# Instance normalization over long rows: 8 MB tiles in three buffers, loads and stores in one fixed order on one queue

## The chip, the cores and the metric

One core of one Trainium2 chip. Times are device microseconds (us) of one execution; a median is over the runs of one kernel. The work is the same in both kernels, so a lower time is better. I call "ring" the line of transfers that one issuing engine has handed to the core's 16 DMA engines; q1 in the profile is SyncE's, q10 ScalarE's. In profile lines DVE is VectorE, ACT ScalarE, POOL GpSimd and SPq the queue of SyncE.

## The reference

```python
# x: (256, 256, 4096) float32
mean = np.mean(x, axis=2, keepdims=True)
var = np.var(x, axis=2, keepdims=True)
return ((x - mean) / np.sqrt(var + eps)).astype(np.float32)
```

65,536 rows of 16 KB are read once and written once: 1073.7 MB each way.

## The kernel before

Each tile is 128 partitions x 2 rows (4 MB), in six buffers. SyncE issues the loads, ScalarE the stores.

```python
K = 2
BUFS = 6
x_t = x_flat.rearrange("(t p k) d -> t p k d", p=P, k=K)
# ... out_t likewise; pools io (BUFS), small (2 * BUFS), singles
for i in range(ntiles):
    x_tile = io.tile([P, K, d], mybir.dt.float32)
    nc.sync.dma_start(out=x_tile, in_=x_t[i])
    # ... stats, mv, rstd, nbias from the pool small
    for r in range(K):
        for j in range(nsub):                       # nsub = 8 pieces of 512
            nc.vector.bn_stats(out=stats[:, r, j, :], in_=xr[:, r, j, :])
        nc.vector.bn_aggr(out=mv[:, r, :], in_=stats[:, r])
    # ... one square root, reciprocal and bias product for both rows
    for r in range(K):
        nc.scalar.activation(out=x_tile[:, r, :], in_=x_tile[:, r, :], func=Identity,
                             bias=nbias[:, r : r + 1], scale=rstd[:, r : r + 1])
    nc.scalar.dma_start(out=out_t[i], in_=x_tile)
```

## Time and profile before

| | before |
|---|---|
| time, median of the first three runs | 5180.87 us (5179.3 to 5187.5) |
| VectorE, ScalarE busy | 51%, 38% |
| 16 DMA engines busy | 99.2% of the span |
| bytes moved over the span | 415 GB/s |

### The profile page before, as it was taken

What the parts mean: (1) busy time and instruction counts of PE and PEld (TensorE: products, weight loads), DVE (VectorE), ACT (ScalarE), POOL (GpSimd) and SP (SyncE); (2) the same over time, 40 slices, a digit from 0 to 9 for tenths busy, and PEclk for the clock granted to TensorE, in tenths of its full rate; (3) what the DMA queues carried; (4) which work ended last, traced back from release to release, by engine and by line L of the source; (5) the groups of instructions that cost most, each with busy time, mean ns of one, the idle gap of its engine ahead of it and who ended that gap; (6) DMA issues with size and microseconds to landing.
All of it is one profiled execution on the core that took longest, in us unless ns stands there. A gap on an engine that the chain in (4) does not pass through costs nothing.

```text
span 5180.7 us, 7450 instructions
## 1 busy us (share of the span) xinstructions
DVE 2654.0 (51%) x5121; ACT 1967.0 (38%) x769; POOL 0.2 (0%) x4
## 2 busy tenths in 40 slices
DVE  6544555554455555444555554455555445555543
ACT  3333333433333433433343433333343333334334
POOL 0000000000000000000000000000000000000000
DMA  9999999999999999999999999999999999999998
GB/s 425 412 410 413 420 417 422 417 414 416 410 416 413 417 418 414 413 412 417 417 416 418 413 414 418 410 417 420 417 415 417 417 413 417 417 419 415 415 416 367
DMA packets 73786, 2147.99 MB, mean 415 GB/s; under 512 B 8192, under 2 KB 8192, under 8 KB 8192
## 3 DMA queue, kind: packets, MB, share of 16 engines
q1 hardware_dynamic: 36864, 1073.76, 49.7%
q10 hardware_dynamic: 36864, 1073.76, 49.5%
q14 instruction: 58, 0.48, 0.0%
HBM read 1073.74 MB, written 1073.74 MB: 415 GB/s over the span
## 4 chain that ended last, share of the span: by engine, by line
DMA 69%; DVE 17%; ACT 7%; issue 6%; another core or an unknown queue 0%; SPq 0%
DMA x_tile<-in_x_dram 43%; DMA out_dram<-x_tile 26%; DVE stats L55 16%; ACT x_tile L77 7%; DVE mv L56 1%; DVE nbias L67 0%; SPq L46 0%; DVE rstd L65 0%; ACT rstd L58 0%
## 5 line engine op out<-in xcount | busy, mean ns | idle before, releaser
L55 DVE BATCH_NORM_STATS2 stats<-x_tile 128x6 f32<-128x512 f32 x4096 | 2464.1, 674 | 2460.3 <-DMA x_tile<-in_x_dram 2460.3
L77 ACT ACTIVATE x_tile<-x_tile,nbias,rstd 128x4096 f32<-128x4096 f32 x512 | 1917.8, 3793 | 3172.3 <-DVE nbias L67 3172.3
L56 DVE BATCH_NORM_AGGREGATE mv<-stats 128x2 f32<-128x48 f32 x512 | 185.7, 363 | 8.8
L58 ACT ACTIVATE rstd<-mv,eps_tile 128x2 f32<-128x2 f32 x256 | 71.7, 280 | 23.9 <-DVE mv L56 23.9
L67 DVE SCALAR_TENSOR_TENSOR nbias<-mv,rstd 128x2 f32<-128x2 f32 x256 | 41.0, 160 | 8.8
L65 DVE RECIPROCAL rstd<-rstd 128x2 f32<-128x2 f32 x256 | 27.7, 108 | 23.6 <-ACT rstd L58 23.6
L58 ACT ACT_TABLE_LOAD x1 | 1.3, 1283 | 0.7 <-PEq L101 0.7
L42 DVE MEMSET eps_tile<- 128x1 f32 x1 | 0.1, 59 | 0.8 <-PEq L101 0.8
L101 POOL MEMSET const-bfloat16-1.0<- 128x1 bf16 x1 | 0.1, 101 | 0.0
L101 POOL MEMSET const-uint8-127<- 128x1 uint8 x1 | 0.1, 101 | 0.0
L101 POOL MEMSET const-float32-0.0<- 128x1 f32 x1 | 0.1, 98 | 0.2 <-issue 0.2
L101 POOL MEMSET const-float32-1.0<- 128x1 f32 x1 | 0.1, 98 | 0.0
## 6 DMA issues: line engine op xcount, KB each, us to landing
x_tile<-in_x_dram SPq DMA_DIRECT2D x256, 4096.0 KB, 23.7
out_dram<-x_tile ACTq DMA_DIRECT2D x256, 4096.0 KB, 18.6
```

The lines of the kernel that those rows point to most:

```text
L42: nc.vector.memset(eps_tile, eps)
L55: nc.vector.bn_stats(out=stats[:, r, j, :], in_=xr[:, r, j, :])
L56: nc.vector.bn_aggr(out=mv[:, r, :], in_=stats[:, r])
L58: nc.scalar.activation(out=rstd, in_=mv[:, :, 1], func=mybir.ActivationFunctionType.Sqrt, bias=eps_tile, scale=1.0,)
L65: nc.vector.reciprocal(out=rstd, in_=rstd)
L67: nc.vector.scalar_tensor_tensor(out=nbias, in0=mv[:, :, 0], scalar=-1.0, in1=rstd, op0=mybir.AluOpType.mult, op1=mybir.AluOpType.mult,)
L77: nc.scalar.activation(out=x_tile[:, r, :], in_=x_tile[:, r, :], func=mybir.ActivationFunctionType.Identity, bias=nbias[:, r : r + 1], sca ...
L101: nc = _bacc.Bacc("TRN2", target_bir_lowering=False, num_devices=1)
```

## The change

Its intent: long runs in one direction, 64 KB contiguous per partition, and an order of transfers that doesn't depend on which of two rings happens to be served. Rows are finished one by one, and the store of a tile stands in SyncE's queue between two loads.

```diff
-    K = 2
-    BUFS = 6
+    K = 4
+    BUFS = 3
+    AHEAD = 2
...
+    def row(x_tile, r):      # statistics, rstd, nbias and normalization of one row
...
+    def finish(i):
+        x_tile = tiles.pop(i)
         for r in range(K):
-            nc.scalar.activation(... nbias[:, r : r + 1], scale=rstd[:, r : r + 1])
-        nc.scalar.dma_start(out=out_t[i], in_=x_tile)
+            row(x_tile, r)
+        nc.sync.dma_start(out=out_t[i], in_=x_tile)
+
+    for i in range(AHEAD):
+        load(i)
+    for i in range(ntiles):
+        finish(i)
+        if i + AHEAD < ntiles:
+            load(i + AHEAD)
```

More of the change, by code (lines that the diff above doesn't have):

```diff
@@ L25 @@
     n, d = x_flat.shape
-    rows_per_tile = P * K
-    assert n % rows_per_tile == 0
-    ntiles = n // rows_per_tile
+    ntiles = n // (P * K)
+    assert n == ntiles * P * K
     x_t = x_flat.rearrange("(t p k) d -> t p k d", p=P, k=K)
     out_t = out_flat.rearrange("(t p k) d -> t p k d", p=P, k=K)
-    BN_FMAX = nc.vector.BN_STATS_FMAX
-    nsub = (d + BN_FMAX - 1) // BN_FMAX
-    assert d % BN_FMAX == 0
+    FMAX = nc.vector.BN_STATS_FMAX
+    nsub = d // FMAX
+    assert d == nsub * FMAX
     io = ctx.enter_context(tc.tile_pool(name="io", bufs=BUFS))
-    small = ctx.enter_context(tc.tile_pool(name="small", bufs=2 * BUFS))
+    small = ctx.enter_context(tc.tile_pool(name="small", bufs=8))
     singles = ctx.enter_context(tc.tile_pool(name="singles", bufs=1))
@@ L42, with load @@
     nc.vector.memset(eps_tile, eps)
-    for i in range(ntiles):
+    tiles = {}
+    def load(i):
         x_tile = io.tile([P, K, d], mybir.dt.float32)
         nc.sync.dma_start(out=x_tile, in_=x_t[i])
-        stats = small.tile([P, K, nsub, 6], mybir.dt.float32)
-        mv = small.tile([P, K, 2], mybir.dt.float32)
-        rstd = small.tile([P, K], mybir.dt.float32)
-        nbias = small.tile([P, K], mybir.dt.float32)
+        tiles[i] = x_tile
+    def row(x_tile, r):
         xr = x_tile.rearrange("p k (s f) -> p k s f", s=nsub)
-        for r in range(K):
-            for j in range(nsub):
-                nc.vector.bn_stats(out=stats[:, r, j, :], in_=xr[:, r, j, :])
-            nc.vector.bn_aggr(out=mv[:, r, :], in_=stats[:, r])
+        stats = small.tile([P, nsub, 6], mybir.dt.float32)
+        mv = small.tile([P, 2], mybir.dt.float32)
+        rstd = small.tile([P, 1], mybir.dt.float32)
+        nbias = small.tile([P, 1], mybir.dt.float32)
+        for j in range(nsub):
+            nc.vector.bn_stats(out=stats[:, j, :], in_=xr[:, r, j, :])
+        nc.vector.bn_aggr(out=mv, in_=stats)
         nc.scalar.activation(
             out=rstd,
-            in_=mv[:, :, 1],
+            in_=mv[:, 1:2],
             func=mybir.ActivationFunctionType.Sqrt,
@@ L68 @@
             out=nbias,
-            in0=mv[:, :, 0],
+            in0=mv[:, 0:1],
             scalar=-1.0,
@@ L74 @@
         )
-        for r in range(K):
-            nc.scalar.activation(
-                out=x_tile[:, r, :],
-                in_=x_tile[:, r, :],
-                func=mybir.ActivationFunctionType.Identity,
-                bias=nbias[:, r : r + 1],
-                scale=rstd[:, r : r + 1],
-            )
-        nc.scalar.dma_start(out=out_t[i], in_=x_tile)
+        nc.scalar.activation(
+            out=x_tile[:, r, :],
+            in_=x_tile[:, r, :],
+            func=mybir.ActivationFunctionType.Identity,
+            bias=nbias,
+            scale=rstd,
+        )
+    def finish(i):
+        x_tile = tiles.pop(i)
+        for r in range(K):
+            row(x_tile, r)
[6 more added lines that the diff above has]
+            load(i + AHEAD)
 _INS = ['x', 'eps']
```

## The prediction

> **What bounds the kernel now.** I read the busy shares and the queue part of the page first, because they say which resource is full; then the waits, to see whether anything but that resource is waited for; then stretches of time, to see where the full resource is not at its best; last the packet records of the trace, one by one.
>
> ```profile
> DVE 2654.0 (51%) x5121; ACT 1967.0 (38%) x769; POOL 0.2 (0%) x4
> ...
> DMA  9999999999999999999999999999999999999998
> ...
> q1 hardware_dynamic: 36864, 1073.76, 49.7%
> q10 hardware_dynamic: 36864, 1073.76, 49.5%
> ...
> HBM read 1073.74 MB, written 1073.74 MB: 415 GB/s over the span
> ```
>
> VectorE and ScalarE are half idle. The 16 DMA engines are busy 49.7 + 49.5 = 99.2% of the span: q1 carries the loads (issued by SyncE), q10 the stores (issued by ScalarE). 2147.5 MB have to move and neither kernel can move less. So the time can fall only in two ways: the 0.8% in which engines are idle, or a shorter busy time per byte. A busy share of 99% doesn't say that the second is exhausted.
>
> ```profile
> ACT x_tile L77 <- DVE nbias L67: 3172.3, 256, 27.9
> DVE stats L55 <- DMA x_tile<-in_x_dram: 2460.3, 254, 23.9
> ...
> SPq L46 <- DMA out_dram<-x_tile: 4914.6, 248, 33.2
> ```
>
> VectorE waits for loads, and SyncE's queue (second view, the queue's own waits) waits 248 times for a store to land and free a buffer. Six buffers are always full: compute isn't the limit, and each load starts just when a store has ended. That last point matters below.
>
> ```profile
> 12.00:31.00 19.00, 17.55 (x33) 7.30 (x3) 0.00 (x0) 1.00 1.02 442
> ...
> 5126.00:5140.00 14.00, 6.15 (x15) 7.68 (x3) 0.00 (x0) 1.00 0.00 0
> 5141.00:5179.00 38.00, 0.65 (x4) 22.00 (x8) 0.00 (x0) 1.00 1.00 428
> 100.00:5100.00 5000.00, 2581.18 (x4979) 1896.61 (x742) 0.00 (x0) 1.00 0.99 416
> ```
>
> These are stretches of the trace; the last column is GB/s. The steady part runs at 416 GB/s, while the opening loads (no store about) and the closing stores (no load about) run faster. (442 is too high by the granularity of packets that straddle the window's ends.) Between 5126 and 5140 us nothing moves: the last loads' compute is waited for.
>
> **Packets.** The trace's DMA records list 65,536 data packets of 32 KB, each with a duration. The commonest by far is 1213 ns: 56,182 packets are within 3 ns of it, for loads, stores, and stretches where each engine alternates load, store, load. In the opening, where six loads stand in line on one ring, the completion write of one load follows that of the one before by 9.681 us on each engine: 8 packets, 433 GB/s over 16 engines, with no gap at the border of two DMAs. The floor of this program at that pace is 512 DMAs of 4 MB x 9.681 = **4957 us**. The difference to 5181 I account for so: the sum of all durations above 1213 ns, divided by 16, is 164 us (156 of it in 4,636 packets that took 1.75 us on average), and the time in which fewer than 16 packets are in flight is 61 us, of which 14.6 are the hole before 5141, some 3.5 the start and the end, and about 42 short gaps. 4957 + 164 + 61 = 5182.
>
> When do the long packets come? Lined up on the issues, nearly all lie 4 to 8 us after a load or a store was issued, as its first packets start. The first store of all is issued at 31.5 us; the loads of all 16 engines average 1803 ns at 34.0 us, the store packets begin at 35.3, and from then on load and store packets alternate at 1213. Around 2012 us a load joins a stretch with stores only, and the store packets then average 2057 ns. But a load issued at 2026.8, while the previous load was still on that ring, begins at 2034 with no long packet. So I read the cost as that of a ring that starts from empty beside a busy one, not as that of changing direction: around 2016 to 2023 nearly all 16 engines change direction together every packet and stay at 1213.
>
> **What the Trainium skill says.** (1) "DMA: Bandwidth & Descriptors", section "Measured", gives 425 GB/s for 16 MB transfers, and "Where 436 GB/s comes from" a ceiling of 435.2. The trace's 433 inside runs of loads agrees; 416 over the steady part is the gap that can be had, 4%. (2) The same page, "Queues, rings and completion order": every engine goes round-robin between the rings that have work, packet by packet. The trace agrees (alternation of q1 and q10). It names no cost for a ring that wakes up; the 164 us are this case's. (3) "Perfetto Trace Analysis", section "DMA Optimizations", advises loads on one issuing engine and stores on another, which the kernel does and the change undoes; nothing in this trace shows a gain from it while the buffers are all full.
>
> **The change, part by part.**
> *One ring.* All 256 issues of 8 MB go through SyncE. The built order is: three loads, two stores, then load, store, load, store. Store i waits for the compute of tile i; load i+2 stands behind it and waits for store i-1. Does the ring run empty? Let load i land at T. Store i-1 then runs T to T+19.4, load i+1 from there to T+38.7. Compute of tile i: a row takes 5.11 us of VectorE (16 statistics and 2 aggregates took 13.02 to 23.24 us, halved), plus its reciprocal and bias product, together about 5.4; four rows 21.6; then square root, reciprocal, product and the last 3.8 us activation, about 4.9. So store i is issued at T+26.5, 12 us before the ring would be empty, and load i+2 directly after, because store i-1 landed at T+19.4. A store's first packet needs some 4 us after issue (31.5 to 35.3). 12 covers it, so the ring never empties after the opening and each DMA starts behind a running one. By the reading above, that removes most of the 164 us and the 42 of short gaps.
> *Fewer, larger DMAs.* 256 rather than 512, and perhaps 64 KB packets. With 6 ns lost at a border this is worth next to nothing itself.
> *Compute.* ScalarE makes 512 square roots rather than 256 (256 x 0.28 = 72 us more), VectorE 512 more small operations of 0.11 to 0.16 us (about 70 us). Both lie beside the transfers: 21.5 us of VectorE per tile against 38.7 of DMA.
> *Ends.* Start 2.2 us as before. At the end the last load lands at T, store 126 ends at T+19.4, store 127 is issued at T+26.5 and moves about 1.5 us later: a hole of 8.6 us, then 19.4 and 1.3 to finish. Before, the hole was 14.6.
> *Sum.* Loads 256 x 9.681 = 2478; stores at the 9.725 us that the closing stores took, 2490; together 4968. Plus 2.2 + 8.6 + 1.3 = 4980. I add 8 us for remnants of long packets at 255 changes of direction (0.03 us each). **4988 us**, 3.7% less.
>
> **Rivals.** *A: the long packets belong to the change of direction after all.* Measured there: load joining stores about 1.1 us, store joining loads 0.6. With 128 of the first and 127 of the second, 217 us come back: 4980 + 217 = 5197, the same time. For it: every long stretch I looked at is also where the direction mix changes. Against: the free alternation and the free start at 2034. A half way (0.3 us per change) makes 5057. *B: the fixed order starves the ring.* SyncE issues in order, so a late store holds up a load that could go. If compute took 12 us more, each lost us would cost 128; VectorE's and ScalarE's durations vary by far less. At an overrun of 1 us: 5108. *C: 64 KB rows suit the memory worse, or lose to a coarser split.* Partition starts move from 32 to 64 KB apart; the profile before can't tell; 1% would be 50 us. *D: hidden anyway.* The engines are 99% busy, so no gain but the end's 6 us: 5175. This takes the busy share for efficiency, and the packets speak against it.
>
> **Range and chances.** The floor with its ends is 4957 + 12 = 4969, a little less if packets of 64 KB save something; I set the low end at 4962. The threshold of 2% is 5077. I give my reading, with up to 0.1 us per change, about 72%; a part of A (0.1 to 0.35 us) or C some 14%, still under 5077; A in full, B or D 13%; slower needs A and B together, 1%. So 0.86 / 0.13 / 0.01, range 4962 to 5075.
>
> **What would show it.** Right: GB/s of 428 to 433 in every slice between the ends, packets at twice 1213 ns (or still 1213) with hardly any long ones, all bytes on q1, SyncE's queue waiting mostly for ScalarE's last activation, idle time of VectorE about 18 us per tile, a hole of 8 to 9 us before the last store. Wrong: a dip or long packets at every change of direction (A), moments without any packet in each tile (B), all packets longer by a per cent (C). The prediction fails if the ring does empty, or if the first packet after a change of direction waits for the end of the one before.

## More of the kernel before

All runs told here were fast runs by the state recorded with them, and the granted clock was 1.000.

From the page of the kernel before: the data rate in 40 equal slices of the span, and the row of DMA queue 14 (packets, MB, share).

```profile
GB/s 425 412 410 413 420 417 422 417 414 416 410 416 413 417 418 414 413 412 417 417 416 418 413 414 418 410 417 420 417 415 417 417 413 417 417 419 415 415 416 367
...
q14 instruction: 58, 0.48, 0.0%
```

The first slice, which holds the only long stretch of loads without stores, is the fastest; those after it, but for the last, lie 2.5 to 5.3% below the 433 that the prediction works out for undisturbed packets.

## The result, and the profile after

| | before | after |
|---|---|---|
| median of 4 runs each | 5180.09 us | 5016.2 us (5007.2 to 5019.7) |
| ratio | | 0.966, 95% interval 0.962 to 0.970 |
| rate over the span | 415 GB/s | 428 GB/s |

Ratios here and below are the mean time of one kernel's fast runs over that of the other's in the same rounds, so not quite the ratio of the medians. The predicted time was 4988 us with a range of 4962 to 5075; the measured one is 28 us above the prediction.

The page of the changed kernel (the same parts as before):

```profile
span 5018.0 us, 7844 instructions
...
DVE 2667.3 (53%) x5633; ACT 2083.6 (42%) x1025; POOL 0.2 (0%) x4
...
GB/s 426 432 432 432 433 433 434 434 434 433 427 432 429 426 432 430 427 434 427 427 427 432 428 426 433 429 427 429 430 428 427 428 432 427 427 432 428 427 432 362
...
q1 hardware_dynamic: 36864, 2147.50, 99.7%
q14 instruction: 61, 0.50, 0.0%
HBM read 1073.74 MB, written 1073.74 MB: 428 GB/s over the span
```

All data is on q1. After the first slice and up to 1250 us (ten slices) the rate is 432 to 434 GB/s; the prediction had 428 to 433 for every slice between the ends. Then it varies from 426 to 434. The waits of the compute engines and of SyncE's queue (waiter, what it waited for, us in total, times, longest):

```profile
ACT rstd L60 <- DVE mv L59: 2483.6, 130, 36.6
DVE stats L58 <- DMA x_tile<-in_x_dram: 2228.2, 126, 34.6
```

```profile
SPq L88 <- ACT x_tile L76: 3233.2, 128, 26.6
SPq L88 <- DMA x_tile<-in_x_dram: 1631.0, 126, 20.5
SPq L48 <- DMA out_dram<-x_tile: 22.3, 2, 12.2
```

SyncE's queue no longer waits for stores to land (22 us against 4915 before). It waits for ScalarE to finish a tile, as predicted. One tile in the timeline of the changed kernel, start and duration of each:

```profile
2035.80 5.44 DVE L58 BATCH_NORM_STATS2 stats<-x_tile 128x6 f32<-128x512 f32 x9 [17.35 <-DMA x_tile<-in_x_dram]
...
2057.41 3.80 ACT L76 ACTIVATE x_tile<-x_tile,nbias,rstd 128x4096 f32<-128x4096 f32 x1 [0.42 <-DVE nbias L68]
2061.24 0.34 SPq L88 DMA_DIRECT2D out_dram<-x_tile  x1
2061.67 0.38 SPq L48 DMA_DIRECT2D x_tile<-in_x_dram  x1
```

From the load's landing to the store's issue: 2061.2 - 2035.8 = 25.4 us, where 26.5 was predicted. Stretches of time (busy times of the engines, granted clock, DMA share, GB/s):

```profile
100.00:1000.00 900.00, 477.28 (x1007) 367.99 (x182) 0.00 (x0) 1.00 1.00 433
1500.00:4900.00 3400.00, 1808.27 (x3820) 1411.63 (x695) 0.00 (x0) 1.00 1.00 429
4978.00:4997.00 19.00, 13.82 (x30) 15.96 (x7) 0.00 (x0) 1.00 0.11 48
4998.00:5016.00 18.00, 0.00 (x0) 0.00 (x0) 0.00 (x0) 1.00 0.94 408
```

The hole before the last store is 19 us long, more than twice what was predicted, and 0.11 of DMA share shows that a few engines still worked in it.

**Where the 28 us are.** Three quantities of the packet records account for a span: what the packets take undisturbed, what they take above that ("long packets", summed and divided by 16), and the time for which packets are missing ("gaps": 16 less the packets in flight, summed over time and divided by 16). The prediction calls its 61 us of this "the time in which fewer than 16 packets are in flight"; counted in that way it would be 155 us, but its sum is right with the 61. Packets are now 64 KB and take 2418 ns; one 8 MB DMA follows another by 19.32 us where nothing disturbs.

| term, us | predicted | measured |
|---|---|---|
| 256 DMAs, undisturbed | 4968 | 4946 |
| start and end | 3.5 | 3.1 |
| long packets | 8 | 50 |
| hole before the last store and other gaps | 8.6 | 20 |
| sum | 4988 | 5019 (span 5018.0) |

The profiled run took 5019.7 us, a little more than the median, so these terms differ by 31 us and not by 28.

**Engines drift apart.** The long packets lie almost all at the border of two DMAs (after 1250 us, 91% of their time is in the last packet of the earlier one), and only 6 of the 50 us come before 1250 us. I followed each DMA engine through the records (which don't name it) by joining the end of each packet to the start of the next. In the records each engine ends its part of a DMA with a packet of 4 bytes; I call it the completion write, and the distance from the first of the 16 to the last the lag. After the first load the lag is 0.5 us. After 300 us one engine is 5 us behind the first one, after 1250 us 11 to 12 us, and there it stays to the end; about nine engines remain within 0.5 us of each other. 12 us is just the slack of the fixed order. A load has landed only when the slowest engine has written its part (where VectorE waited for a load it started 0.3 to 0.5 us after the last completion write, and in the median 12.3 us after the first), so the store of that tile is issued late for the fast engines: from 1250 us on a store was issued in the median 1.2 us before the fastest engine ran out of work. Two questions follow, which the experiments take up: what drove the 164 us of long packets before, and what makes an engine lag.

### The profile page after: what moved, and what is told of

Read it like the earlier page. It is cut to its first block, busy times and chain, and to the rows that moved or that the text cites. A ratio compares the mean times of both kernels' runs of the same rounds, so it can differ in the third digit from the quotient of the medians.

```text
span 5018.0 us, 7844 instructions
## 1 busy us (share of the span) xinstructions
DVE 2667.3 (53%) x5633; ACT 2083.6 (42%) x1025; POOL 0.2 (0%) x4
## 3 DMA queue, kind: packets, MB, share of 16 engines
q1 hardware_dynamic: 36864, 2147.50, 99.7%
## 4 chain that ended last, share of the span: by engine, by line
DVE 45%; another core or an unknown queue 43%; ACT 9%; DMA 1%; issue 1%; ACTq 0%
DVE stats L58 41%; ACT x_tile L76 9%; DVE mv L59 2%; DMA x_tile<-in_x_dram 1%; DVE rstd L67 1%; DVE nbias L68 1%; ACT rstd L60 1%; ACTq L60 0%
## 5 line engine op out<-in xcount | busy, mean ns | idle before, releaser
L58 DVE BATCH_NORM_STATS2 stats<-x_tile 128x6 f32<-128x512 f32 x4096 | 2506.3, 674 | 2228.2 <-DMA x_tile<-in_x_dram 2228.2
L76 ACT ACTIVATE x_tile<-x_tile,nbias,rstd 128x4096 f32<-128x4096 f32 x512 | 1945.7, 3800 | 403.5 <-DVE nbias L68 403.5
L60 ACT ACTIVATE rstd<-mv,eps_tile 128x1 f32<-128x1 f32 x512 | 148.8, 291 | 2508.5 <-DVE mv L59 2483.6
L67 DVE RECIPROCAL rstd<-rstd 128x1 f32<-128x1 f32 x512 | 74.8, 146 | 87.5 <-ACT rstd L60 87.3
L68 DVE SCALAR_TENSOR_TENSOR nbias<-mv,rstd 128x1 f32<-128x1 f32 x512 | 75.2, 147 | 4.3
```

The lines of the kernel that those rows point to most:

```text
L58: nc.vector.bn_stats(out=stats[:, j, :], in_=xr[:, r, j, :])
L60: nc.scalar.activation(out=rstd, in_=mv[:, 1:2], func=mybir.ActivationFunctionType.Sqrt, bias=eps_tile, scale=1.0,)
L67: nc.vector.reciprocal(out=rstd, in_=rstd)
L68: nc.vector.scalar_tensor_tensor(out=nbias, in0=mv[:, 0:1], scalar=-1.0, in1=rstd, op0=mybir.AluOpType.mult, op1=mybir.AluOpType.mult,)
```

## The experiments

Twelve kernels ran, four each on three chips; the kernel before ran beside each of them, with medians of 5187, 5196 and 5187 us. Diffs are against the changed kernel.

### two_queues: stores back on ScalarE's ring

```diff
-        nc.sync.dma_start(out=out_t[i], in_=x_tile)
+        nc.scalar.dma_start(out=out_t[i], in_=x_tile)
```

> The changed kernel, but with stores issued by ScalarE on its own ring: 8 MB tiles, 64 KB rows and three buffers kept, the fixed order and the single ring undone. Ring theory (the time went when a second ring woke beside a busy one): most of the loss returns, 256 DMAs at about 0.35 us for a ring that starts plus short gaps, 5060 to 5180 us, with long packets at the starts of DMAs. Size theory (large DMAs and 64 KB rows are what helped): about 5016 us, within 0.4% of the changed kernel.

Measured: 5466.5 us, ratio to the kernel before 1.052 (1.048 to 1.056). Neither theory had it: large tiles on two rings are slower than the kernel before. The queue's own waits:

```profile
SPq L48 <- DMA out_dram<-x_tile: 5305.0, 125, 79.7
```

With three buffers each load waits for a store to land, up to 80 us. Compared with the issues, 251 of the 256 DMAs were issued after the previous one on their ring had ended on the first engine. Long packets sum to 207 us, and gaps to 306 us. So the size theory falls, and of the change's parts the tile size by itself would have been a loss.

### small_one_queue: old tiles, one ring

```diff
-    K = 4
-    BUFS = 3
-    AHEAD = 2
+    K = 2
+    BUFS = 6
+    AHEAD = 4
```

> The changed kernel with the old geometry: 4 MB tiles, 32 KB rows, six buffers, loads four tiles ahead, all on one ring. The order leaves some 38 us of slack before the ring runs dry, where the changed kernel leaves 12. Size theory: back to about 5180 us. Ring theory with 0.17 us lost at every change of direction, as the changed kernel showed on average: 512 changes make 87 us, 4946 + 87 + ends of 12 = 5045 us. Slack theory (in the changed kernel the lost time is that of stores issued too late for the engines that are ahead): hardly any long packets, about 4975 us.

Measured: 5032.8 us (5016.8 to 5056.7), ratio 0.969 (0.966 to 0.973). The gain is there with the old tiles, so the ring and the order make it, not the size. The page of this kernel:

```profile
GB/s 421 432 432 434 432 434 433 433 434 432 434 433 433 434 432 433 433 433 434 432 433 433 432 434 433 433 433 432 434 432 433 433 432 434 433 432 427 419 411 302
```

433 GB/s until 4500 us, with long packets of 0.2 to 0.4 us in each 500 us after the first, in spite of twice the changes of direction. Then it breaks down: from 4500 to 5000 us they are 14.6 us, and at the end a few engines finish while the others wait. The slack theory was right about the long packets and wrong about the time: with 38 us of slack the engines drift further before anyone waits, and the bill comes at the end.

### rows_apart: 16 KB contiguous instead of 64 KB

```diff
-    x_t = x_flat.rearrange("(t p k) d -> t p k d", p=P, k=K)
+    x_t = x_flat.rearrange("(t k p) d -> t p k d", p=P, k=K)
```

(and the same for the output)

> The changed kernel with the four rows of a partition taken 128 rows apart, so 16 KB contiguous per partition instead of 64 KB, same 8 MB DMAs, ring, order and buffers. If 64 KB rows matter, slower by 1% or more (over 5066 us). If they don't: 5016 us within 0.4%, with the same floor per DMA, 19.32 us.

Measured: 5035.6 us (5032.3 to 5042.0), ratio 0.969 (0.966 to 0.973), where the changed kernel has 0.966 and, repeated, 0.964. 20 us, 0.4%, is on the edge of what I had called no effect, and one part of the expectation missed: where nothing disturbs, one DMA follows another by 19.44 us, not 19.32. In undisturbed stretches the rates are 431 GB/s with 16 KB packets, 433 with 32 KB (small_one_queue) and 434 with 64 KB (few_instr below). Contiguity is worth a few tenths of a per cent here.

### half_stats: less compute, more slack (wrong result)

```diff
-        for j in range(nsub):
+        for j in range(nsub // 2):
```

(with `stats` half as long)

> The changed kernel with statistics over half of each row (wrong result on purpose), so that a tile's compute falls from 26.5 to some 18 us and the slack before the ring runs dry grows from 12 to about 20 us. Slack theory: the average of long packets falls from 52 to below 30 us and the hole before the last store to a few us: 4970 to 4990 us. Slow-engine theory (one DMA engine loses about 0.4 us at each pair of changes of direction by itself and sets the pace): long packets of the slowest engine stay at some 50 us, the spread between engines grows to some 20 us, and the time falls only by the compute's part of the hole, 4995 to 5010 us.

Measured: 4995.3 us (4990.9 to 4997.4), ratio 0.961 (0.959 to 0.964). Two stretches of this kernel:

```profile
800.00:2800.00 2000.00, 556.77 (x1430) 824.01 (x412) 0.00 (x0) 1.00 1.00 434
3000.00:4900.00 1900.00, 534.77 (x1372) 782.59 (x392) 0.00 (x0) 1.00 1.00 430
```

Both theories were partly right: long packets fell to 24 us in all, as the slack theory had it, and the time lies in the range of the other. The lag grows through the first 2900 us to 15 us, at 434 GB/s with long packets of 0.2 to 0.8 us in each 500 us after the first; there the slack is used up, the lag stays at 15 to 16 us, the rate falls to 430 and long packets rise to 3 to 5 us in each 500 us. So more slack delays the loss, but something drives the engines apart at a steady pace, some 4.5 us in 1000 us.

The clean stretch shows what. From 750 to 2850 us the lag rises from 5.1 to 14.7 us in twelve steps of 0.75 to 0.96 us, and between them it stands still to within 0.1 us. Each step falls in the DMA in which one of the 18 packets of queue 14 (8 KB each, 0.31 us long) ran, and the steps come about every 180 us, so these twelve hit one and the same engine, the slowest. Not all long packets are explained so: those over 60 ns too long sum to 11.6 us over the engines, of which 7.2 us directly follow a packet of queue 14; the other 4.4 us lie in a few clusters on several engines and don't move the lag. (The expectation of few_instr below, written after this run, calls the packets at fetches "the only long packets"; that was too strong.)

The Trainium skill, "CRC Debugging", section "Comparing the Two Runs", names queue 14 as the instruction-refill DMAs, and "Perfetto Trace Analysis", section "The 4-stage abstract model", gives 64 bytes to an instruction. The numbers agree: the changed kernel's 7844 instructions x 64 B are 61.3 x 8 KB, and its queue 14 has 61 packets; VectorE's 3585 instructions in half_stats make 28 refills, one per 178 us. The lagging engine is the one that fetches VectorE's program, as the spacing says; the records don't say so themselves. In the changed kernel the lag does the same from 300 to 1200 us: eight of eleven refills, 110 to 119 us apart, bring steps of 0.6 to 0.9 us, 6.0 of the 6.5 us by which it grows there, and VectorE's 5633 instructions make one refill per 114 us. Of the 5.4 us of the first 300 us, at most 3.5 come in DMAs with a refill.

### after_again: the changed kernel repeated

No edit; a yardstick on the second chip.

> The changed kernel once more, unaltered, as the yardstick for the other runs of this chip: 5016 us within 0.3%, one DMA engine some 12 us behind the first one from about 1200 us on.

Measured: 5017.8 us (5013.7 to 5022.0), ratio 0.964 (0.961 to 0.967); lag 12 us from 1250 us on; long packets 44 us.

### few_instr: no statistics (wrong result)

```diff
-        for r in range(K):
-            row(x_tile, r)
+        nc.scalar.activation(out=x_tile, in_=x_tile, func=Identity, bias=eps_tile, scale=1.0)
```

> The changed kernel without statistics (wrong result on purpose): one ScalarE activation over the whole tile, constant scale and bias. The traces show that in the quiet stretches the only long packets are those that an 8 KB instruction fetch runs into, some 0.7 us each, and that the fetches of VectorE's program come to the same DMA engine each time. This kernel has some 10 fetches instead of 61, and 25 us of slack. Fetch theory: hardly any drift between the engines, hardly any long packets, 434 GB/s in all slices, 4946 + 3 of ends + 5 = 4955 us. Direction theory (each change of direction costs 0.17 us on average, or 0.4 us per pair on the slow engine): 4990 to 5000 us, as half_stats.

Measured: 4959.4 us (4958.7 to 4959.9), ratio 0.953 (0.950 to 0.956); the direction theory falls. Its page:

```profile
GB/s 423 435 433 433 435 433 432 433 436 434 432 437 434 432 436 435 433 435 435 433 434 436 433 434 436 433 434 436 433 432 437 434 432 436 434 433 436 435 432 414
...
q14 instruction: 5, 0.04, 0.0%
```

With 253 changes of direction on one ring, long packets sum to 4.3 us, nearly all in the first 700 us; the lag grows to 6.5 us by 800 us, and after that it doesn't move for 4100 us. A store is issued 17.7 us before the fastest engine runs dry. This run also has less compute than the changed kernel, so it doesn't separate refills from slack alone; but half_stats had nearly this slack and drifted, with 45 refills. The drift of the first 800 us isn't at refills (the first one of this kernel comes at 996 us), and I can't explain it; long packets of 3 to 4 us in the first 500 us occur in several of these kernels.

### more_instr: 8192 instructions that nobody waits for

```diff
         nc.vector.bn_aggr(out=mv, in_=stats)
+        for _ in range(16):
+            nc.gpsimd.tensor_copy(out=idle, in_=mv[:, 0:1])
```

> The changed kernel plus 16 one-element GpSimd copies per row, 8192 in all, that nobody waits for: some 64 more instruction fetches, 0.5 MB more of traffic. Fetch theory: the DMA engine that fetches GpSimd's program loses some 64 x 0.7 = 45 us, more than VectorE's one (44 x 0.7 = 31), so the slowest engine is some 14 us slower, and more engines wait on each other: 5025 to 5045 us. Direction theory and slack theory: 5016 us within 0.2%, because nothing that is waited for has changed.

Measured: 5025.8 us (5021.4 to 5028.4) beside 5017.8 (5013.7 to 5022.0) of after_again on the same chip; ratios 0.966 and 0.964, whose intervals overlap. Queue 14 has 134 packets instead of 61, and long packets rise from 44 to 53 us. The direction is that of the fetch theory and the size is at its lower edge: 8 us for 73 refills. It also lies within the 0.2% that the other theories allowed, so this run doesn't decide between them. Two engines lag nearly alike here (10.2 and 9.1 us at 800 us, where the changed kernel has 9.1 and 5.0), so the lag is shared, not added. I count this as agreeing, not as proof.

### store_rows: a store for each row

```diff
             row(x_tile, r)
-        nc.sync.dma_start(out=out_t[i], in_=x_tile)
+            nc.sync.dma_start(out=out_t[i][:, r], in_=x_tile[:, r, :])
```

> The changed kernel with each row's store (2 MB, 16 KB per partition) issued as soon as that row is normalized, on the same ring; correct result. The first row of a tile is stored some 10 us after its load landed instead of 26.5, so the slack grows from 12 to some 28 us and there is no hole before the last stores but that of the engines that lag. Slack and fetch theory together: long packets rare until the lag reaches 28 us, 4946 + 10 (smaller store packets) + 3 + 30 of the slowest engine = 4985 to 4995 us. If every change of DMA on a ring costs something: 640 DMAs instead of 256, over 5030 us.

Measured: 5059.1 us (5037.6 to 5086.9), ratio 0.972 (0.968 to 0.977). A miss: I expected 4990. Two stretches:

```profile
1500.00:3000.00 1500.00, 807.04 (x1706) 632.02 (x312) 0.00 (x0) 1.00 1.00 433
3500.00:4900.00 1400.00, 724.88 (x1533) 569.47 (x280) 0.00 (x0) 1.00 0.99 415
```

The slack holds until about 3100 us at 433 GB/s, so 640 DMAs instead of 256 cost nothing while the ring is full. When the slack is used up, the rate is worse than the changed kernel's 429. I read it so: each tile now has four stores at which the fast engines can run dry, not one. Fine stores buy a later start of the loss and a steeper one.

### small_two_queues: the row order alone

```diff
-    K = 4
-    BUFS = 3
-    AHEAD = 2
+    K = 2
+    BUFS = 6
+    AHEAD = 4
...
-        nc.sync.dma_start(out=out_t[i], in_=x_tile)
+        nc.scalar.dma_start(out=out_t[i], in_=x_tile)
```

> The kernel before (4 MB tiles, six buffers, loads on SyncE's ring, stores on ScalarE's) with only the row by row order of the statistics and normalization taken from the change. Ring theory: the time of the kernel before comes from rings that start from empty and from loads that wait for a store to land; row order alone leaves that, 5130 to 5190 us, long packets near 164 us. Compute-order theory (the gain came from finishing a row at once, where the kernel before puts a tile's reciprocal behind the next tile's statistics): about 5020 to 5060 us.

Measured: 5192.4 us, ratio 0.9996 (0.998 to 1.001): the same as the kernel before. Finishing rows one by one is worth nothing here. Long packets fell to 115 us and gaps rose to 118 us, which is the same sum as before (164 and 61) within 8 us.

### copy_two_queues: two rings, hardly any compute (wrong result)

As small_two_queues, with few_instr's single activation for the compute.

> As small_two_queues, but without statistics (wrong result on purpose): one ScalarE activation per tile, some 7 us, so that nearly all six buffers stand in one of the two rings and compute holds none. If a ring costs time only where it starts from empty, and both rings now hold a DMA in reserve: 4965 to 5050 us and long packets well below 164 us. If two rings with loads beside stores cost time by themselves, however early the issue: 5100 us or more.

Measured: 4968.6 us (4968.5 to 4968.6), ratio 0.955 (0.951 to 0.958). Page, and the queue's own waits:

```profile
GB/s 422 435 432 434 434 431 435 433 433 435 431 435 433 433 435 431 434 433 433 435 431 434 434 432 435 432 433 434 431 435 432 434 434 431 435 432 433 435 431 411
```

```profile
SPq L48 <- DMA out_dram<-x_tile: 4762.0, 250, 31.9
```

Long packets sum to 1.9 us. So loads beside stores on two rings cost nothing by themselves, and a load that waits for a store to land (4762 us of waiting, as in the kernel before) costs nothing by itself either. The difference is when the issue comes: here no load and one store came after the previous DMA on its ring had ended on the first engine. In the kernel before, 82 loads and 97 stores did.

### tiny_two_queues: two rings, 2 MB tiles in twelve buffers

```diff
-    K = 4
-    BUFS = 3
-    AHEAD = 2
+    K = 1
+    BUFS = 12
+    AHEAD = 8
```

(and stores on ScalarE, as above, with 16 small buffers)

> As small_two_queues with tiles of 2 MB in twelve buffers, correct result: the same memory, finer grain, two rings. Where rings start from empty: 1024 DMAs instead of 512, so 5180 us or more. If the finer grain keeps a DMA in reserve on both rings: 5000 to 5080 us.

Measured: 5578.0 us, ratio 1.072 (1.068 to 1.077). 579 of the 1024 DMAs were issued to a ring that had ended; long packets 414 us, gaps 183 us. Over the five kernels with two rings:

| kernel | issued to an ended ring | long packets, us | gaps, us | median, us |
|---|---|---|---|---|
| copy_two_queues | 1 of 512 | 2 | 9 | 4968.6 |
| small_two_queues | 144 of 512 | 115 | 118 | 5192.4 |
| before | 179 of 512 | 164 | 61 | 5180.1 |
| two_queues | 251 of 256 | 207 | 306 | 5466.5 |
| tiny_two_queues | 579 of 1024 | 414 | 183 | 5578.0 |

Long packets follow the count, at 0.7 to 0.9 us each. (A DMA issued just before its ring ends is late too, and isn't counted, so this isn't the exact cost of one. In the kernel before, the median store comes only 0.2 us before that end; with the 0.34 us of the issue itself added, 146 stores are late and not 97.)

Kernels differ in more than this count, so I also compared the DMAs of one kernel, the kernel before, giving each packet that is over 60 ns too long to the DMA whose first packet starts nearest. The 82 loads that came after their ring had ended have 1.1 us of long packets each; the other 173 have 0.03 us. That is the claim itself, for loads, and it accounts for 89 of the 164 us. Stores divide less cleanly: 0.2 us for the 85 that came over 0.5 us late, 0.5 us for the 81 that were issued 0.5 to 4 us before their ring ended.

### lean: a version to beat both

One ring, 4 MB tiles in six buffers with loads four ahead, as small_one_queue, and statistics in few instructions:

```diff
+        nc.vector.reduce_sum(out=tot, in_=x_tile, axis=mybir.AxisListType.X)
+        for r in range(K):
+            nc.scalar.activation(out=junk, in_=x_tile[:, r, :], func=Square,
+                                 accum_out=sq[:, r : r + 1])
+        nc.vector.tensor_scalar_mul(nmean, tot, -1.0 / d)
+        nc.vector.tensor_mul(m2, nmean, nmean)
+        nc.vector.scalar_tensor_tensor(out=m2, in0=sq, scalar=1.0 / d, in1=m2,
+                                       op0=mult, op1=subtract)
...     # square root with eps, reciprocal, nbias = nmean * rstd, Identity per row
```

> A version meant to beat both kernels, correct result: one ring and fixed order as in the change, 4 MB tiles in six buffers with loads four ahead (38 us of slack), and statistics from one row sum on VectorE and one squared sum per row on ScalarE, so that VectorE's program falls from 5633 to about 1540 instructions. Fetch theory: VectorE's fetching DMA engine loses 14 x 0.7 = 10 us instead of 31; 4957 + 3 + 4 + 10 + a hole of 9.5 before the last store = 4984 us, within 4975 to 5000. If fetches don't matter: 5015 to 5055 us, as small_one_queue.

Measured: 4977.7 us (4977.1 to 4980.6), correct, ratio 0.957 (0.954 to 0.960), below the 0.964 and 0.966 of the changed kernel. Its page:

```profile
DVE 2432.0 (49%) x1537; ACT 3893.9 (78%) x1794; POOL 0.2 (0%) x4
...
GB/s 420 431 432 433 433 433 433 434 432 433 433 434 432 433 433 433 434 433 433 432 434 434 432 433 432 434 432 433 433 433 434 432 433 432 434 433 433 433 433 393
...
q14 instruction: 38, 0.31, 0.0%
```

Long packets sum to 4.6 us in all. ScalarE is twice as busy as before and that costs nothing. Compared with small_one_queue, which has the same ring, order and tiles, this is 55 us less (on another chip; the ratios to the kernel before are 0.957 and 0.969); what differs is the statistics, and with them VectorE's 1537 instead of 5633 instructions. The slack isn't what differs: from 200 to 1000 us a store is issued in the median 35.5 us before the fastest engine runs dry in lean and 35.6 us in small_one_queue. After 2000 us it is 30 and 14 us. The kernel lean takes the variance as the mean of squares less the square of the mean, which was accurate enough for these inputs and would not be for rows with a large mean.

## Why the prediction was right, and which terms were not

- **"A busy share of 99% doesn't say that the second is exhausted."** Right: the changed kernel's engines are 99.7% busy as well, with 3% more bytes per second.
- **A ring that starts from empty costs, a change of direction doesn't.** Right: few_instr has 4 us of long packets with 253 changes of direction on one ring, copy_two_queues 2 us with two full rings, and in the kernel before the late loads have 1.1 us each where the others have 0.03. For late loads, 89 of the 164 us, this is shown within one kernel; for stores it rests on the count over kernels. Rival A, a cost at every change, falls.
- **One ring and a fixed order keep a DMA in reserve.** Right for the first 1250 us, at 433 GB/s. The step that failed is "12 covers it, so the ring never empties after the opening": I treated the 16 engines as one. A store is issued when the slowest engine has landed its load, and has to be there when the fastest needs it; engines drifted apart until the 12 us were used up, for the most part by instruction refills that fell on one of them. This is a form of rival B, which I had tied to varying compute. In place of 8 us of long packets there were 50, and in place of a hole of 8.6 us one of 19, about as much longer as the lag. Two of the prediction's own signs came out wrong with it: long packets were not "hardly any", and some slices fell to 426 or 427 GB/s.
- **Stores at 9.725 us per 4 MB** (2490 us in the sum): too much. On one ring both kinds follow each other by 19.32 us per 8 MB, 22 us less in all, which hid a part of the other two errors: without this the time would have been missed by some 50 us and not by 28, so the closeness is in part luck.
- **Fewer, larger DMAs are worth next to nothing.** Right for size on its own: small_one_queue keeps nearly all of the gain with 4 MB tiles, and two_queues loses with 8 MB. 64 KB packets are worth about 0.2% against 32 KB by the intervals between completion writes (19.32 against 2 x 9.681 us). Rival C was smaller than its 1% and of the other sign.
- **Compute lies beside the transfers.** Right in its size (25.4 us per tile against 26.5). Compute matters through the slack that it leaves and, unforeseen, through its count of instructions.
- **Rival D** (hidden anyway) falls with the result.
- Two readings were loose, without effect on the sum: the first store packet starts at 35.8 us and not at 35.3, so 4.3 us after its issue, and the built order has 251 changes of direction, not 255.

What stays open: the drift in the first 300 to 800 us that isn't at refills; what the late stores cost; which engine fetches which program (inferred from the spacing); why 73 more refills in more_instr moved the time by only 8 us, where one on the slowest engine moves the lag by 0.8; and why small_one_queue's runs scatter by 40 us where lean's scatter by 4.

## What to carry to other kernels

Where the DMA engines are nearly always busy, look at the durations of their packets and at the time between an issue and the end of the previous DMA on that ring: loads that came too late beside stores stretched packets here, and the busy share hid it. Order loads and stores so that each ring always holds one more DMA, and count the slack from the slowest engine's landing to the fastest engine's last packet. In a program of thousands of unrolled instructions the refills themselves set the engines apart, so fewer instructions can shorten a transfer-bound kernel: 55 us between small_one_queue and lean, though 8192 more on GpSimd cost the changed kernel some 8 us.

## What the Trainium skill lacked or had wrong

- "DMA: Bandwidth & Descriptors", "Queues, rings and completion order": no word on a DMA issued to a ring that has run empty. Here long packets came to 0.7 to 0.9 us per such issue; 164 us in the kernel before, 2 us with the same two rings kept full.
- "Perfetto Trace Analysis", "DMA Optimizations", says that separate issuing engines for loads and stores may make sense. It made no difference while both rings stayed full (433 GB/s on two rings in copy_two_queues, 433 on one in lean), and with compute between load and store one ring in fixed order was better (5032.8 against 5192.4 us for the same tiles).
- No page that I read tells what instruction refills cost the data DMAs: some 0.8 us each for the engine hit, in half_stats, and twelve of 18 on one engine. "Runtime: NRT & Kernel Launch", "Terms", says that refills come in 16 KiB blocks; the packets of queue 14 here are 8,192 B, and 61 of them carry the changed kernel's 7844 instructions.
- No page that I read says that the lag between the 16 engines grows under a long stream ("DMA: Bandwidth & Descriptors", "Latency and other measured facts", only remarks that two of them are usually slower, and guesses that this is tied to DMAs issued from GpSimd): 0.5 us after the first load, 12 us after 1250 us in the changed kernel.
- No page that I read gives a rate on this chip for packets of 16 to 64 KB; the size still shows: 431, 433 and 434 GB/s for 16, 32 and 64 KB packets in undisturbed stretches.
